# A decoder layer in float32 on one core: the input first, gate logits and two key tiles chunk by chunk in turn, and the per-layer embedding projection moved to the end

## The chip, the core and the metric

The kernel runs on one core of one Trainium2 chip. The metric is device time in microseconds (us) of one execution. The core has a matrix engine (TensorE, PE in the profile; its weight loads are listed apart as PEld), a vector engine (VectorE, DVE), a scalar engine (ScalarE, ACT), a general engine (GpSimd, POOL) and a sync engine (SP) that here issues all the DMA transfers. Each engine runs its own instruction list in order and waits for the others through semaphores. SBUF is the on-chip memory of 128 partitions, PSUM the memory into which PE writes, DRAM the memory off the core.

## What is computed

One layer of a hybrid decoder, for a prompt of 1024 tokens and 64 sample tokens (8 sequences of 8), with a model width of 1024, in float32. The reference, cut to what matters:

```python
proj = rmsnorm(h, norm_mix) @ w_in
qkv, z, b_logit, a_logit, sq, sk, sv, gates = jnp.split(proj, cuts, axis=-1)
o_a = gdn_branch(...)   # causal conv of width 4 + silu on q, k, v; l2norm of q and k;
                        # beta = sigmoid(b_logit), g = -exp(a_log)*softplus(a_logit + dt_bias);
                        # gated delta rule in chunks of 64 with a triangular solve; 8 heads
o_b = swa_branch(...)   # sliding-window attention, 16 heads of 64, window 128
h = h + (sigmoid(gates[:D]) * o_a + sigmoid(gates[D:]) * o_b) @ w_out
h = h + relu(rmsnorm(h, norm_ffn) @ w_up)**2 @ w_down
h = h + sigmoid(rmsnorm(h, norm_ple) @ w_ple_gate) * (p_l @ w_ple_proj)
```

The last line is the per-layer embedding: `p_l` (256 features a token) times `w_ple_proj` (256 by 1024) needs nothing but inputs, and is called PLE below.

## The kernel before

**Numbers and tiles.** Features lie on the partitions, tokens along the rows. The T = 1088 tokens are cut into chunks `CH` of 384, 384 and 320 columns; the 1024 features are KT = 8 tiles of 128, the k tiles. Each float32 operand is split in two rounded halves, x = xh + xl and w = wh + wl, and a product is three matmuls: xh by wh (L166), xl by wh (L167), xh by wl (L168). One output tile of 128 features (one f) is 8 k tiles x 3 chunks x 3 = 72 such matmuls.

**Weights.** A list `order` fixes the order in which weight tiles of 512 KB are streamed: `w_load` issues the DMA into `wr` (three buffers), `w_split` copies the high half on ACT (`wh`, L134) and subtracts on POOL (`wl`, L135; for the first two tiles on DVE), into two buffers each. `next_w` hands out a split tile and sets the next load and split going.

**Order.** The program is written for a tile scheduler that sets the order on each engine from the program text and the tiles' buffers. The start, however, is laid out by hand: a tuple of steps runs the eight PLE tiles `ple(0)` to `ple(7)` in between the steps of the three input norms n0, n1, n2.

**The start.** The inputs `pT` are loaded and split (`phi`, `plo`, L286 and L287). A PLE tile is 2 k tiles x 3 chunks x 3 = 18 matmuls (L166 to L168 with `phi` and `plo`), 144 for all eight. Each is copied out of PSUM by ACT, times 0.5, into `ppo` (L328; four buffers) and stored to DRAM (`ppd`, L332, 544 KB each). `x_norm(i)` handles chunk i of the input: ACT squares it (L306), DVE adds the eight k tiles up (L309), `rsqrt_pe` sums over the partitions by one-column matmuls (`psn`, L247), DVE scales (L250), POOL takes the power -0.5 (L251), DVE builds diagonal tiles (`dg`, L256), and PE spreads them over the partitions (`pst`, L257). Then per k tile DVE multiplies by the norm (L316), ACT rounds off the high half (`xh`, L317), POOL or, for two of eight, DVE subtracts (`xl`, L318).

**Gates, keys, solve.** After the norms come the gate logits `ba` (48 matmuls, L388), their transposes (L427), a chain of small DVE steps from logits to the decay `g` (L401 to L422), and PE's cumulative sums of g (L435 on). Then a loop over the eight heads h computes the key tile of each: `conv_steps` (72 matmuls, copies out of PSUM into `raw`, four conv steps on DVE with `cacc`, L511), `key_rows` (the decay rows `E`, one buffer) and `key_products` (k by k matmuls, L591, multiplied by E on DVE and copied by ACT into `kk` and `kb`, L593, stored to DRAM). After the last head DVE solves the triangular systems row by row (`fs`, L666, and `LT`, L667) while PE goes on with the projections of the attention; the attention's key and query halves (`klo`, L888; `qst`, L901) are DVE steps queued among the solve's rows, and PE's first score matmuls (`psc`, L930 and L931) read them.

**The end.** After the attention, the delta rule, `w_out` and the MLP (8 blocks; the last block's `w_down` tiles feed `next_operand`, which makes the last norm's operand `ph`, `pl`, with L200, and adds up squares in `acc`, L1388), the gate of the PLE is one projection: f = 0 to 7, 72 matmuls each. f = 0 runs its chunks in turn (`inter=True`) while `col_rsqrt_pe` makes the norm's scale from `acc`. Per f a buffer `B` is loaded from `ppd`, and per chunk DVE multiplies by the norm's scale (L1450), ACT takes the tanh (L1451), DVE multiplies by the PLE tile (L1452) and adds to h (L1454), and SP stores the result (L1455).

## Time and profile before

| what | value |
|---|---|
| time, median of 3 runs (lowest, highest) | 2139.82 us (2135.79, 2142.8) |
| the profiled execution: its own time | 2146.7 us |
| its span | 2144.9 us |
| TensorE clock granted, mean over the span | 0.983 of full speed |
| PE busy | 2079.6 us |
| DVE, ACT, POOL busy | 1071.9, 795.5, 718.0 us |
| DMA moved | 196.50 MB |

The profiled execution is one run: its time is 6.9 us above the median of the three, and its span lacks 1.8 us of its time. A row of a timeline has the start in us, the duration, the engine, the source line, the operation, the tiles written and read, how many instructions the row holds, and in brackets the idle time before it and what ended that. Matmuls overlap: the distance between the starts of two matmuls in a row is what one costs, not its duration.

### The profile page before, as it was taken

The numbers are of one execution on the slowest core, as the hardware profiler recorded it, in microseconds if no ns is written. First come the engines' busy times: TensorE is split into PE (matmuls) and PEld (weight loads), VectorE is DVE, ScalarE is ACT, GpSimd is POOL, SyncE is SP. The second block draws the span as 40 slices with busy tenths as digits, with TensorE's granted clock in tenths as the row PEclk, the third lists the DMA queues.
The fourth block names the chain that finished last, engine by engine and source line by source line (L and its number), as shares of the span: only waits on it lengthen the run. The fifth ranks groups of instructions, "written<-read, shape, count | busy, mean of one in ns | idle before, by whom it ended". The sixth has DMA issues, their size and how long they took to land.

```text
span 2144.9 us, 33830 instructions
## 1 busy us (share of the span) xinstructions
PE 2079.6 (97%) x13597; PEld 1995.2 (93%) x13597; DVE 1071.9 (50%) x1717; ACT 795.5 (37%) x1951; POOL 718.0 (33%) x676
## 2 busy tenths in 40 slices
PE   6999999789999999999999999999999999999999
PEld 6899899668889999999998999999999999999999
DVE  6444499787654555445555444233332323333654
ACT  6476433477643443344334322212131212212411
POOL 3332456243235545454455222212121212121211
PEclk9999999899999999999999999999999999999999
DMA  6365443343243223322242221111111111111132
GB/s 238 122 216 183 116 147 109 104 125 114 85 142 97 76 93 123 108 92 77 93 151 75 77 69 50 40 50 40 50 40 50 40 50 41 49 43 47 40 127 80
DMA packets 89065, 196.50 MB, mean 92 GB/s; under 512 B 33613, under 2 KB 44749, under 8 KB 88781
## 3 DMA queue, kind: packets, MB, share of 16 engines
q1 hardware_dynamic: 88908, 194.35, 27.7%
q8 instruction: 107, 1.75, 0.3%
q14 instruction: 50, 0.40, 0.1%
HBM read 145.48 MB, written 50.78 MB: 91 GB/s over the span
## 4 chain that ended last, share of the span: by engine, by line
PE 80%; DVE 11%; ACT 4%; issue 3%; POOL 2%; DMA 1%; SPq 0%; ACTq 0%; DVEq 0%; POOLq 0%
PE ps L166 23%; PE ps L168 22%; PE ps L167 22%; DVE fs L666 3%; DVE LT L667 3%; PE psn L975 1%; PE pst L953 1%; DVE nm L938 1%; PE psc L1285 1%; ACT pst L572 1%; PE psc L1216 1%; PE psn L1297 1%; PE psc L1290 1%; PE psc L1280 1%; ACT pr L940 1%
## 5 line engine op out<-in xcount | busy, mean ns | idle before, releaser
L135 POOL TENSOR_TENSOR wl<-wr,wh 128x1024 fp32r<-128x1024 f32 x140 | 343.4, 2453 | 909.1 <-ACT wh L134 893.8
L166 PE MATMUL ps<-xh,wh 128*128 128x384 f32 (+1 forms) x1800 | 621.9, 345 | 3.0 <-ACT qf L350 1.6
L167 PE MATMUL ps<-xl,wh 128*128 128x384 f32 (+1 forms) x1800 | 600.1, 333 | 0.0
L168 PE MATMUL ps<-xh,wl 128*128 128x384 f32 (+1 forms) x1800 | 596.7, 332 | 0.0
L166 PEld LDWEIGHTS ps<-xh,wh 128*128 128x128 f32 x1800 | 343.1, 191 | 15.9 <-issue 11.1
L167 PEld LDWEIGHTS ps<-xl,wh 128*128 128x128 f32 x1800 | 343.9, 191 | 1.2 <-issue 1.1
L168 PEld LDWEIGHTS ps<-xh,wl 128*128 128x128 f32 x1800 | 342.1, 190 | 1.6 <-issue 0.7
L134 ACT ACTIVATE wh<-wr 128x1024 fp32r<-128x1024 f32 x143 | 150.8, 1054 | 518.2 <-PE ps L167 441.3
L166 PE MATMUL ps<-uh,wh 128*128 128x384 f32 (+1 forms) x768 | 251.2, 327 | 1.2 <-DVE h L1436 1.2
L168 PE MATMUL ps<-uh,wl 128*128 128x384 f32 (+1 forms) x768 | 251.3, 327 | 0.0
L167 PE MATMUL ps<-ul,wh 128*128 128x384 f32 (+1 forms) x768 | 251.0, 327 | 0.0
L1436 DVE TENSOR_TENSOR h<-h,ps 128x384 f32<-128x384 f32 (+1 forms) x192 | 100.6, 531 | 226.3 <-PE ps L168 226.3
L166 PE MATMUL ps<-ph,wh 128*128 128x384 f32 (+1 forms) x600 | 197.9, 330 | 0.0
L167 PE MATMUL ps<-pl,wh 128*128 128x384 f32 (+1 forms) x600 | 197.6, 329 | 0.0
L168 PE MATMUL ps<-ph,wl 128*128 128x384 f32 (+1 forms) x600 | 197.5, 330 | 0.0
L1422 DVE TENSOR_TENSOR ul<-us,uh 128x384 fp32r<-128x384 f32 (+1 forms) x96 | 98.0, 1022 | 115.2 <-ACT uh L1421 115.2
L166 PEld LDWEIGHTS ps<-uh,wh 128*128 128x128 f32 x768 | 144.3, 188 | 2.0 <-DVE h L1436 2.0
L168 PEld LDWEIGHTS ps<-uh,wl 128*128 128x128 f32 x768 | 144.3, 188 | 0.0
L167 PEld LDWEIGHTS ps<-ul,wh 128*128 128x128 f32 x768 | 144.2, 188 | 0.0
L511 DVE SCALAR_TENSOR_TENSOR cacc<-raw,cw,cacc 128x1112 f32<-128x1112 f32 x72 | 111.1, 1543 | 62.0 <-ACT cacc L509 60.7
L1420 ACT ACTIVATE us<-ut 128x384 f32<-128x384 f32 (+1 forms) x96 | 48.2, 502 | 196.0 <-DVE ut L1419 194.5
L1419 DVE SCALAR_TENSOR_TENSOR ut<-ps,rb 128x384 f32<-128x384 f32 (+1 forms) x96 | 51.3, 535 | 136.5 <-PE ps L168 136.5
(413 smaller groups left out, 3410.4 us busy)
## 6 DMA issues: line engine op xcount, KB each, us to landing
wr<-win SPq DMA_DIRECT2D x60, 512.0 KB
wr<-wup SPq DMA_DIRECT2D x32, 512.0 KB
wr<-wdn SPq DMA_DIRECT2D x32, 512.0 KB
ppd<-ppo SPq DMA_DIRECT2D x8, 544.0 KB
kTd<-kT SPq DMA_DIRECT2D x8, 544.0 KB
Ed<-E SPq DMA_DIRECT2D x8, 544.0 KB
rg<-Ed SPq DMA_DIRECT2D x8, 544.0 KB
gkT<-kTd SPq DMA_DIRECT2D x8, 544.0 KB
```

The costliest lines, as they stand in the source:

```text
L134: act(hv, rv, AF.Copy)
L135: (nc.gpsimd if i > 1 else nc.vector).tensor_tensor(lv, rv, hv.bitcast(F32), ALU.subtract)
L166: mm(ps[:M, :w], a, h[:, c0 : c0 + w], start=(k == 0), stop=False)
L167: mm(ps[:M, :w], a, l[:, c0 : c0 + w], start=False, stop=False)
L168: mm(ps[:M, :w], b, h[:, c0 : c0 + w], start=False, stop=(k == n - 1))
L511: stt(out=cc, in0=raw[:, j : j + CONVW], scalar=cw[:, f, j : j + 1], in1=cc, op0=ALU.mult, op1=ALU.add)
L666: tt(tmp, X[:, j : j + 1, j + 1 :].broadcast_to(sh), X[:, 0:j, j : j + 1].broadcast_to(sh), ALU.mult)
L667: tt(X[:, 0:j, j + 1 :], X[:, 0:j, j + 1 :], tmp, ALU.add)
L1419: stt(out=t, in0=ps[:, :w], scalar=0.0, in1=rb2[:, c0 : c0 + w], op0=ALU.max, op1=ALU.mult)
L1420: act(s, t, AF.Square)
L1422: tt(lo[:, c0 : c0 + w], s, hi[:, c0 : c0 + w].bitcast(F32), ALU.subtract)
L1436: tt(hc, hc, ps[:, :w], ALU.add)
```

## The change

- **Weights.** The two PLE weight tiles `wpp` leave the head of the list and stand ahead of the last block's four `wdn` tiles; `wba` (the gate logits' weights) comes third, behind two key weights. Its split goes to a tile `wn` of its own. The PLE weights are split into buffers of the `xh` and `xl` kind, free by then.
- **Start.** SP issues chunk 0 of the input first, then the constants, one key weight, chunk 1, a key weight, chunk 2, `wba`. The PLE is gone from here. The norm n0 is followed by `turn(0)`, then n1, `turn(1)`, n2, `turn(2)`. A turn holds three PSUM tiles and for each of the 8 k tiles issues three matmuls for key tile 8, three for key tile 9 and two for the gate logits, all on chunk i (64 matmuls a turn, 192 in all). Then ACT copies the three tiles out. The key loop's first two heads do only what is left (`conv_rest`).
- **Key loop.** `E` has two buffers. `kb` is gone, ACT writes its copy into half of `kk`. `key_products` stands behind the loop's second step, not its first.
- **End.** `pT` is loaded and split in the last MLP block, behind the PLE weights. `ple(f)` writes its 18 matmuls' result into three PSUM tiles (two of `psc`, one of `pst`) that stay there; `ple(0)` stands ahead of `col_rsqrt_pe`, `ple(f)` ahead of the gate's tile f. The multiplication by the PLE tile reads PSUM; the factor 0.5 moves into the last addition, now a two-operation DVE step. The eight 544 KB stores to `ppd` and the eight loads from it are gone.

The diff, cut to its core:

```diff
-    order = [(d["wpp"][u], 1024) for u in range(2)] + [(d["wba"], 128)]
-    order += [(d["win"][f], 1024) for f in WIN_ORDER]
+    order = [(d["win"][f], 1024) for f in WIN_ORDER]
+    order.insert(2, (d["wba"], 128))
...
+        if b == NUP // 4 - 1:
+            ple_order = len(order)
+            order += [(d["wpp"][u], 1024) for u in range(2)]
+        order += [(d["wdn"][b, u], 1024) for u in range(4)]
...
+                if 0 <= i - ple_order < 2:
+
+                    hi, lo = (xp.tile([P, T], F32R, name=z, tag=t)[:, :1024] for z, t in (("wph", "xh"), ("wpl", "xl")))
...
+    ba = ep.tile([P, T], F32, name="ba", tag="qraw", bufs=1)[:32]
+    raw0 = [ep.tile([P, RAWW], F32, name="raw0", tag="tg") for _ in range(2)]
...
         for i, (c0, w) in enumerate(CH):
...
+            for k in (0, 4):
+                dma(x_in[i][:, k : k + 4], d["xT"][k : k + 4, :, c0 : c0 + w].rearrange("k p t -> p k t"))
+            if i == 0:
+                load_constants()
                 w_load()
...
+            else:
+                w_load()
+        dma(cache, d["cachec"])
...
-        for step in (0, 1, 2, n0, n1, n0, n0, 3, n1, n2, n1, 4, 5, n2, n2, 6, 7):
-            if isinstance(step, int):
-                ple(step)
-            else:
-                next(step, None)
...
+        next(n0)
+        w_split()
+        evacs = [conv_raw(8 + h, raw0[h]) for h in range(2)]
+        keys, (wb, _) = [next_w() for _ in range(2)], next_w()
+        next(n0)
+
+        def turn(i):
+            c0, w = CH[i]
+            c = slice(c0, c0 + w)
+            pk = [pg.tile([P, 512], F32, name="ps", tag="ps") for _ in range(2)]
+            pb = pg.tile([P, 512], F32, name="ps", tag="ps")
+            for k in range(KT):
+                x_h, x_l = (z[:, c] for z in xs[k])
+                for ps, (hi, lo) in zip(pk, keys):
+                    a, b = (z[:, k * P : k * P + P] for z in (hi, lo))
+                    mm(ps[:, :w], a, x_h, start=(k == 0), stop=False)
+                    mm(ps[:, :w], a, x_l, start=False, stop=False)
+                    mm(ps[:, :w], b, x_h, start=False, stop=(k == KT - 1))
+                for j, z in enumerate((x_h, x_l)):
+                    mm(pb[:32, :w], wb[:, k * 32 : k * 32 + 32], z, start=(k + j == 0), stop=(k + j == KT))
+            act(ba[:, c], pb[:32, :w], AF.Copy)
+            for f, ps in zip(evacs, pk):
+                f(c0, w, ps)
+
+        turn(0)
+        next(n1)
+        next(n1)
+        turn(1)
+        next(n2)
+        next(n2)
+        turn(2)
...
-        E = kp.tile([P, T], F32, name="E", tag="E", bufs=1)
+        E = kp.tile([P, T], F32, name="E", tag="E")
...
-        kb = kp.tile([P, 8, 64], F32, name="kb", tag="kb", bufs=1)
...
-            act(kb[64:128, hf * 4 : hf * 4 + 4], ps[64:128].rearrange("p (c f) -> p c f", f=P)[:, :, 0:64], AF.Copy)
+            act(kk[64:128, hf * 4 : hf * 4 + 4, 0:64], ps[64:128].rearrange("p (c f) -> p c f", f=P)[:, :, 0:64], AF.Copy)
...
+        if h < 2:
+            kT = conv_rest(8 + h, raw0[h], kp, key_tile)
+            continue
...
+            wpl, prhs = [next_w() for _ in range(2)], []
+            for k in range(2):
+                pr = B()
+                dma(pr, d["pT"][k])
+                hi = xp.tile([P, T], F32R, name="pph", tag="xh")
+                lo = xp.tile([P, T], F32R, name="ppl", tag="xl")
+                act(hi, pr, AF.Copy)
+                tt(lo, pr, hi.bitcast(F32), ALU.subtract)
+                prhs.append((hi, lo))
...
+    def ple(f):
+
+        res = []
+        for i, (c0, w) in enumerate(CH):
+            ps = pst() if i == 2 else psc()
+            for k, (h_, l_) in enumerate(prhs):
+                a, b = (z[:, k * 512 + f % 4 * P : k * 512 + f % 4 * P + P] for z in wpl[f // 4])
+                mm(ps[:, :w], a, h_[:, c0 : c0 + w], start=(k == 0), stop=False)
+                mm(ps[:, :w], a, l_[:, c0 : c0 + w], start=False, stop=False)
+                mm(ps[:, :w], b, h_[:, c0 : c0 + w], start=False, stop=(k == 1))
+            res.append(ps)
+        return res
+
+
+    first = ple(0)
     col_rsqrt_pe(acc, 1.0 / 1024, EPS, rb2, tp)
...
     for f in range(KT):
-        pr = B()
-        dma(pr, ppd[f])
+        pr = dict(zip((c0 for c0, _ in CH), ple(f) if f else first))
...
-            stt(out=t, in0=t, scalar=1.0, in1=pr[:, c0 : c0 + w], op0=ALU.add, op1=ALU.mult)
+            stt(out=t, in0=t, scalar=1.0, in1=pr[c0][:, :w], op0=ALU.add, op1=ALU.mult)
             hc = hT[f][:, c0 : c0 + w]
-            tt(hc, hc, t, ALU.add)
+            stt(out=hc, in0=t, scalar=0.5, in1=hc, op0=ALU.mult, op1=ALU.add)
```

Three places of the instruction order, before and now. Line numbers of the changed program differ: L257 and L267 there are the old L247 and L257, L394 to L396 the key matmuls, L398 the gate logits.

The first is PE's list where the norm of the second and third chunks is made. Before, the small norm matmuls of the third chunk stand singly among the PLE's matmuls (`phi`, `plo`):

```order
L166 MATMUL ps<-phi,wh 128x384
L257 MATMUL pst<-dg,cst 128x128 x2
L167 MATMUL ps<-plo,wh 128x384
L257 MATMUL pst<-dg,cst 128x64
L168 MATMUL ps<-phi,wl 128x384
```

Now the end of turn 0 and the start of turn 1 stand so:

```order
L394 MATMUL ps<-xh,wh 128x384
L395 MATMUL ps<-xl,wh 128x384
L396 MATMUL ps<-xh,wl 128x384
L398 MATMUL ps<-xh,wn 32x384
L398 MATMUL ps<-xl,wn 32x384
L257 MATMUL psn<-cst,xsq 128x1 x5
L257 MATMUL psn<-cst,xsq 64x1
L267 MATMUL pst<-dg,cst 128x128 x4
L394 MATMUL ps<-xh,wh 128x384 x2
```

The partition sums and the spreading of the second chunk's norm stand together between the turns, with no large matmul between the two.

The second is DVE's list in the triangular solve, where `klo` is queued. Before:

```order
L666 TENSOR_TENSOR fs<-LT 128x572
L667 TENSOR_TENSOR LT<-LT,fs 128x52x11
L666 TENSOR_TENSOR fs<-LT 128x530
L667 TENSOR_TENSOR LT<-LT,fs 128x53x10
L888 TENSOR_TENSOR klo<-klo,khi 128x1024
L666 TENSOR_TENSOR fs<-LT 128x486
```

Now (L681, L682, L903 and L949 are the old L666, L667, L888 and L934):

```order
L681 TENSOR_TENSOR fs<-LT 128x572
L903 TENSOR_TENSOR klo<-klo,khi 128x1024
L682 TENSOR_TENSOR LT<-LT,fs 128x52x11
L681 TENSOR_TENSOR fs<-LT 128x530
L949 SCALAR_TENSOR_TENSOR pr<-psc,rq,tab 128x128
L682 TENSOR_TENSOR LT<-LT,fs 128x53x10
```

`klo` moved ahead of three steps of the solve, and the first score step (`pr`) that follows from it stands two solve steps behind it.

The third is POOL's list ahead of `rks`, a power that the solve waits for. Before:

```order
L135 TENSOR_TENSOR wl<-wr,wh 128x1024 x2
L220 TENSOR_TENSOR nlo<-nsq,nhi 128x384 x2
L790 COPY vss<-vt 64x128
L220 TENSOR_TENSOR nlo<-nsq,nhi 128x320
L220 TENSOR_TENSOR nlo<-nsq,nhi 128x384 x2
L135 TENSOR_TENSOR wl<-wr,wh 128x1024
L220 TENSOR_TENSOR nlo<-nsq,nhi 128x320
L645 TENSOR_TENSOR rks<-rks,pwr 64x8
```

Now (L145, L230, L660 are the old L135, L220, L645):

```order
L145 TENSOR_TENSOR wl<-wr,wh 128x1024 x3
L230 TENSOR_TENSOR nlo<-nsq,nhi 128x384 x2
L805 COPY vss<-vt 64x128
L230 TENSOR_TENSOR nlo<-nsq,nhi 128x320
L230 TENSOR_TENSOR nlo<-nsq,nhi 128x384 x2
L230 TENSOR_TENSOR nlo<-nsq,nhi 128x320
L660 TENSOR_TENSOR rks<-rks,pwr 64x8
```

The weight split that stood two rows ahead of `rks` now stands ahead of all of the `nlo` rows.

More of the change, by code (lines that the diff above doesn't have):

```diff
@@ new lines, in conv_rest @@
+    def conv_rest(f, raw, cvp, dst):
+        rs = raw[:, 3 + NP :].rearrange("p (b t) -> p b t", t=11)
+        nc.gpsimd.tensor_copy(cstate[:, f, 0:3], raw[:, NP : NP + 3])
+        nc.gpsimd.tensor_copy(cstate[:, f, 3:27].rearrange("p (b t) -> p b t", t=3), rs[:, :, 8:11])
+        c = cvp.tile([P, RAWW], F32, name="cacc", tag="cacc", bufs=2)
+        cc = c[:, :CONVW]
+        act(cc, raw[:, 0:CONVW], AF.Copy, scale=cw[:, f, 0:1])
+        for j in range(1, 4):
+            stt(out=cc, in0=raw[:, j : j + CONVW], scalar=cw[:, f, j : j + 1], in1=cc, op0=ALU.mult, op1=ALU.add)
+        th = raw
+        act(th[:, :CONVW], cc, AF.Tanh, scale=0.5)
+        v = lambda z: z[:, NP + 3 : RAWW].rearrange("p (b t) -> p b t", t=11)[:, :, 0:8]
+        if callable(dst):
+            dst = dst()
+        if dst is None:
+            sg = cvp.tile([P, NS], F32, name="sg", tag="sg", bufs=2)
+            stt(out=sg.rearrange("p (b t) -> p b t", t=8), in0=v(th), scalar=1.0, in1=v(c), op0=ALU.add, op1=ALU.mult)
+            stt(out=c[:, :NP], in0=th[:, :NP], scalar=1.0, in1=c[:, :NP], op0=ALU.add, op1=ALU.mult)
+            return c, sg
+        stt(out=dst[:, :NP], in0=th[:, :NP], scalar=1.0, in1=c[:, :NP], op0=ALU.add, op1=ALU.mult)
+        stt(out=dst[:, NP:T].rearrange("p (b t) -> p b t", t=8), in0=v(th), scalar=1.0, in1=v(c), op0=ALU.add, op1=ALU.mult)
+        return dst
@@ L334, in hybrid_layer @@
[L334 to L351 removed]
+            yield
@@ L371, in hybrid_layer @@
     rq, rqs = mp.tile([P, 8, 2, 8], F32, name="rq"), mp.tile([P, NB], F32, name="rqs")
-    ectx = ctx.enter_context(ExitStack())
-    ep = pool(ectx, "ep", 2, side="right")
     kctx = ctx.enter_context(ExitStack())
```

136 lines of the change are left out of this document (42 added, 94 removed).

## The prediction, made before the changed kernel was run

> **What bounds the kernel now.** I read the page's busy times first, PE's list of waits in the start next, then the timelines of PE, ACT, DVE and POOL there, the waits later on, and last the final projection.
>
> ```profile
> PE 2079.6 (97%) x13597; PEld 1995.2 (93%) x13597; DVE 1071.9 (50%) x1717; ACT 795.5 (37%) x1951; POOL 718.0 (33%) x676
> ```
>
> PE is busy 97% of the span. The change removes no matmul: 144 PLE matmuls leave the start and 144 of the same kind come at the end. Only time that PE loses to waits, or to a lower clock, can be won or lost. The list of waits of PE in the first 90 us (us in total, times, longest) shows the losses in the start:
>
> ```profile
> PE ps L166 <- ACT wh L134: 6.7, 1, 6.7
> PE pst L257 <- DVE dg L256: 4.0, 2, 3.4
> PE ps L166 <- ACT ppo L328: 3.3, 1, 3.3
> PE pst L435 <- DVE lg L420: 1.7, 1, 1.7
> ```
>
> Waits cost more than their length, since the matmuls after them run slowly. PE's timeline around two waits, and the granted clock of 70 to 80 us (0.66):
>
> ```profile
> 36.42 0.34 PE L168 MATMUL ps<-phi,wl 128*128 128x384 f32 x1
> 36.60 0.35 PE L166 MATMUL ps<-phi,wh 128*128 128x384 f32 x1
> 37.28 0.30 PE L167 MATMUL ps<-plo,wh 128*128 128x320 f32 x1
> 37.42 0.31 PE L168 MATMUL ps<-phi,wl 128*128 128x320 f32 x1
> ...
> 47.45 1.20 PE L257 MATMUL pst<-dg,cst 128*128 128x128 f32 x4 [3.39 <-DVE dg L256]
> ...
> 52.88 0.48 PE L388 MATMUL ps<-xl,wh 128*32 128x384 f32 x1
> 53.19 0.34 PE L388 MATMUL ps<-xh,wh 128*32 128x384 f32 x1
> ...
> 60.84 0.71 PE L427 MATMUL pst<-cst,ba 32*128 32x32 f32 x6
> ...
> 69.82 0.41 PE L435 MATMUL pst<-g,cst 128*128 128x64 f32 x2 [1.68 <-DVE lg L420]
> ...
> 76.69 0.52 PE L168 MATMUL ps<-xh,wl 128*128 128x384 f32 x1
> 77.58 0.32 PE L166 MATMUL ps<-xh,wh 128*128 128x320 f32 x1
> ```
>
> ```profile
> 70.00:80.00 10.00, 10.00 (x47) 8.66 (x47) 1.81 (x10) 2.74 (x14) 0.00 (x0) 0.66 0.06 16
> ```
>
> Starts lie 0.175 us apart (36.42 to 36.60) for 384 columns and 0.145 for 320 at full clock, and 0.31 (52.88 to 53.19) for 384 in the slow stretches. Each us of slow stretch loses 1 - 0.175/0.31, about 0.45 us. After the 3.39 us gap at 47.45 PE is slow until 53.19, 5.7 us, so 2.6 lost; after the mere 1.68 at 69.82, which small matmuls follow, the last slow row is that of 76.69, another 7 us.
>
> **A: the first 192 large matmuls (+3.2).** Before, 144 PLE and 48 gate-logit matmuls end at 60.84. After, three turns of 64, with the same columns, hold two key tiles and the gate logits. So the two moments compare directly: 192 matmuls are 128 x 0.175 + 64 x 0.145, about 31.7 us at full clock, and before lost 29 of its 61 us. The PLE was what PE could do before the norms; now nothing can. The first rows of that chain, by their nearest rows before:
>
> ```profile
> 4.26 0.84 ACT L286 ACTIVATE phi<-praw 128x768 fp32r<-128x768 f32 x1 [2.26 <-DMA praw<-pT]
> 8.89 1.06 ACT L134 ACTIVATE wh<-wr 128x1024 fp32r<-128x1024 f32 x1 [0.46 <-DMA wr<-wpp]
> 10.98 1.48 ACT L306 ACTIVATE xsq<-xc 128x1536 f32<-128x1536 f32 x1
> 27.76 1.05 ACT L317 ACTIVATE xh<-xc 128x384 fp32r<-128x384 f32 x2 [2.23 <-DVE xc L316]
> ```
>
> ```profile
> 9.99 1.23 DVE L135 TENSOR_TENSOR wl<-wr,wh 128x1024 fp32r<-128x1024 f32 x1 [0.56 <-ACT wh L134]
> 15.51 3.35 DVE L309 TENSOR_TENSOR xsq<-xsq 128x1536 f32<-128x1536 f32 x3 [1.56 <-ACT xsq L306]
> 24.52 0.63 DVE L256 TENSOR_SCALAR dg<-cst,rcomp 128x128 f32<-128x128 f32 x2
> 27.11 1.66 DVE L316 SCALAR_TENSOR_TENSOR xc<-xc,par,pst 128x384 f32<-128x384 f32 x3
> ```
>
> ```profile
> 21.28 2.31 POOL L251 TENSOR_TENSOR rcomp<-rcomp,pwr 128x3 f32<-128x3 f32 x1 [20.86 <-DVE rcomp L250]
> 26.02 0.85 POOL L251 TENSOR_TENSOR rcomp<-rcomp,pwr 128x3 f32<-128x3 f32 x1 [2.43 <-DVE rcomp L250]
> 30.46 3.23 POOL L318 TENSOR_TENSOR xl<-xc,xh 128x384 fp32r<-128x384 f32 x3 [0.36 <-ACT xh L317]
> ```
>
> ```profile
> 25.02 0.73 PE L247 MATMUL psn<-cst,xsq 128*128 128x1 f32 x6
> ```
>
> By 4.26 one piece of `pT` (0.39 MB) had landed, by 8.89 two pieces and two weights (1.8 MB). Chunk 0 of the input is 1.57 MB: its first half is there at about 5.3, all at 8. Squares 1.48, to 9.7; adds 3.35, to 13; sums and scaling 0.9, to 14; the first power 2.3, to 16.3; `dg` twice 0.63, the key weight's split, which DVE's order puts ahead of the third `dg`, 1.23, the third 0.3, spreading 0.5: 19. Multiply and round, 0.55 and 0.52: the first `xh` at about 19.5 to 20. Key 9's weight then holds PE: ACT has it behind three `xh` and a square (to 23.5), DVE's half behind eight multiplications and one `xl` (19 + 8 x 0.55 + 0.6 = 24, and 1.23: 25). POOL's six `xl` at 1.1 each end by 27, ahead of need. So PE is dense from about 25 with 49 matmuls of turn 0 left: 8.5, and some 2 of slow clock as after the gap at 47.45, end at 35.5.
>
> Now the gap between turns: PE's order has the second chunk's partition sums only behind turn 0 and its spreading straight after, and nothing between. Sums 0.73, scaling 0.16, power 0.85, `dg` 0.63, spreading 0.4, multiply 0.55, round 0.52: 3.8 us. Turn 1 starts near 39.4 and takes 11.2 plus 2 slow: 52.5. Behind it stand the third chunk's last spreading and the logits' transposes, then multiply and round; 2 us. Turn 2, 64 x 0.145 = 9.3, ends at 64. That is 3.2 later than 60.84. I put no slow stretch behind the 2 us, since dense matmuls follow at once; the row of 69.82 says that there may be one, and it would cost 2 to 3. Ends: 61 (no slow clock in turns 1 and 2) to 68 (dense from 27, each turn slow for 5.7).
>
> [...]
>
> **B: gates and the first two keys (+2.6).** The group of conv steps, and two rows of POOL, from the solve's start:
>
> ```profile
> L511 DVE SCALAR_TENSOR_TENSOR cacc<-raw,cw,cacc 128x1112 f32<-128x1112 f32 x72 | 111.1, 1543 | 62.0 <-ACT cacc L509 60.7
> ```
>
> ```profile
> 251.14 2.40 POOL L135 TENSOR_TENSOR wl<-wr,wh 128x1024 fp32r<-128x1024 f32 x1 [2.35 <-ACT wh L134]
> ...
> 254.33 1.63 POOL L645 TENSOR_TENSOR rks<-rks,pwr 64x8 f32<-64x8 f32 x1
> ```
>
> Before, PE takes from 60.84 to 77.58 for 48 key matmuls (8.4 us) and about 2 us of small ones: 6.4 lost to the gates. After, key tiles 8 and 9 are done, so PE starts with head 2: its weight waits for a buffer that turn 2 frees (`wh` 1.06, `wl` on POOL 2.40, part of it covered: 1.8); the first key products wait for a conv chain that used to run beside 72 matmuls (1.3); the gates' small steps share DVE with six conv steps of 1.54, so g comes later (2.3) and a slow stretch follows (2.5). With about 1 of smaller waits that is 9 lost, 2.6 more than before. Ends: -2 (head 2 covers all) and +5 (each in full, two slow stretches).
>
> **C: key loop and solve (-4.1).** PE's waits from 61 to 400 us:
>
> ```profile
> PE psc L931 <- DVE klo L888: 7.1, 1, 7.1
> PE psc L591 <- ACT kb L593: 2.6, 2, 1.7
> PE psc L930 <- DVE qst L901: 2.0, 1, 2.0
> ```
>
> ```profile
> 385.21 0.75 DVE L667 TENSOR_TENSOR LT<-LT,fs 128x572 f32<-128x572 f32 x1
> ...
> 386.74 0.71 DVE L667 TENSOR_TENSOR LT<-LT,fs 128x530 f32<-128x530 f32 x1
> ```
>
> `kb`'s waits are those on the copy out of PSUM. Two `E` buffers and the later place of `key_products` can take all 2.6 or none: half, -1.3. The 7.1 + 2.0 before `klo` and `qst` are DVE's queue: DVE is full with the solve, so `klo` comes when the solve's rows ahead of it are done. `klo` moves ahead of three of these (first and last shown, the one between is a multiplication as long as the last): 0.75 + 0.71 + 0.71 = 2.2. The solve waits for `rks`; the 2.40 split that stood before it now stands earlier: up to 2.4. Of 4.6 I take 60%, -2.8, since the third split now holds up `nlo`, which PE's norms wait for. Ends -7.2 and 0.
>
> **D: the end (+0.5).** Of PE's timeline, the first row of gate tile f = 0, the wait in it, and f = 1:
>
> ```profile
> 2034.07 0.34 PE L166 MATMUL ps<-ph,wh 128*128 128x384 f32 x1
> ...
> 2040.13 0.83 PE L247 MATMUL psn<-cst,acc 128*128 128x1 f32 x6 [1.04 <-DVE acc L1388]
> ...
> 2056.71 0.36 PE L166 MATMUL ps<-ph,wh 128*128 128x384 f32 x1
> ```
>
> f = 0 takes 22.6 us for work of 11.9: 10.7 lost, of which only 1.04 is one wait; the rest is small norm matmuls and the slow clock among them. `ple(0)`, 18 matmuls or 3 us, now stands ahead of that and could cover it. But the eight `xh` buffers are now filled by the four operand tiles of the last block's `w_down` and by four of the PLE (two of inputs, two of weights), so the operands of f = 5 to 7 for the gate, which are of that kind, can be written only when the last `w_down` tile has been read. I put them and the sum `acc` 1.5 to 2.5 later; then `ple(0)`'s 3 us are used up and the 10.7 stay. `ple(1)`'s PSUM tiles wait for f = 0's evacuation, 0 to 1.9. The eight stores and eight loads of 544 KB lay beside a busy PE; without them nothing is saved. The multiplication by 0.5 that goes was on ACT, the one that comes rides in DVE's last addition, 0.55 either way. If `acc` isn't later, D is -3; if the buffers hold up PE, +3.
>
> **Sum.** 3.2 + 2.6 - 4.1 + 0.5 = +2.2. The profiled execution took 2146.7 (span 2144.9 and 1.8 around it) and would take 2148.9; it lies 6.9 above the median 2139.82, and from that the forecast is 2142.
>
> **Rivals.**
> - *Turns in full series (slower).* Each norm waits for the turn before, each turn starts slow, and B's waits add up: A +7, B +5, C -4.1, D +0.5: +8.4, 2148. For it: PE's order, and a slow clock after only 1.68 us of idle. Against it: the squares and additions of the later chunks are done early. It decides when turn 2 ends after 67 us.
> - *Shorter waits behind the start (faster).* A 0, B 0, C -7.2, D -1: -8.2, 2132. For it: 9.1 us of waits for DVE's queue, whose order moved the right way. Against it: PE's late start, which no other work covers.
> - *`ple(0)` covers the last norm (faster).* A, B, C as forecast, and D -6 in place of 0.5: -4.3, 2135.5. For it: 3 us of work at full clock ahead of the sums, which keep PE busy while `acc` ends. Against it: the small norm matmuls stay spread among the large ones, and `acc` comes later.
>
> **Chances.** 0.3% of this time, 6.4 us, is about what a measurement can tell from no change. Forecast 0.44 (its terms' ends leave 0.33 within 0.3%, 0.08 slower, 0.03 faster), turns in series 0.26 (0.20 slower, 0.06 within), shorter waits 0.22 (0.19 faster, 0.03 within), covered norm 0.08 (0.05 within, 0.03 faster). That is faster 0.25, within 0.47, slower 0.28. The range runs from rival two's 2132 to rival one's 2148, and beyond each by 2 and 4, the scatter of the three runs (4.0 below and 3.0 above the median): 2130 to 2152.
>
> **What would show it.** In the profile of the changed kernel: first dense turn matmuls near 25, turn 2's end near 64, a gap of 3.8 between turn 0 and 1 with slow pitch after it, the wait on `klo` near 4 in place of 7.1, and 10 to 11 us lost in f = 0. I am wrong if turn 2 ends before 60 or after 68, or if the sum of PE's waits behind 100 us moves by over 6.

## The result: slower by 0.8%, and the profile after

| what | before | after |
|---|---|---|
| median of 5 runs each, side by side on one chip | 2141.92 us | 2158.26 us |
| ratio, with its 95% interval | | 1.0078 [1.0053, 1.0103] |
| the same in two later comparisons | | 1.0056 [1.0035, 1.0078], 1.0069 [1.0045, 1.0093] |
| profiled execution, its span | 2146.7, 2144.9 us | 2160.68, 2158.9 us |

The kernel became 12 to 16 us slower; +2.2 was forecast, and 2158 lies outside the forecast's range. One run of the changed kernel, in the last comparison, took 4041.35 us, and its medians here leave that run out. The busy times of after, for the line shown of before:

```profile
PE 2081.2 (96%) x13597; PEld 1994.9 (92%) x13597; DVE 1069.2 (50%) x1716; ACT 787.5 (36%) x1926; POOL 728.6 (34%) x676
```

PE has the same 13597 matmuls and as good as the same busy time: 1.6 us more, while the span grew by 14.0. What came in this pair of profiles is idle time. The longest of PE's waits of after in its first 100 us (us in total, times, longest):

```profile
PE psn L257 <- DVE xsq L367: 12.3, 1, 12.3
PE ps L395 <- POOL xl L375: 2.7, 1, 2.7
PE ps L394 <- ACT xh L374: 2.6, 3, 1.3
PE pst L267 <- DVE dg L266: 2.4, 4, 1.5
PE ps L398 <- POOL wn L145: 1.2, 1, 1.2
PE ps L178 <- POOL wl L145: 1.0, 1, 1.0
```

PE's timeline of after at the landmarks that the prediction named: the first large matmul, the two waits on POOL, the ends of turn 0 (the `psn` row) and turn 1 (the `pst` row at 56.49), the starts of turns 1 and 2, the last matmul of turn 2, and the last two of the logits' eight transposes behind it.

```profile
18.88 0.69 PE L394 MATMUL ps<-xh,wh 128*128 128x384 f32 x1 [1.26 <-ACT xh L374]
...
26.59 0.65 PE L395 MATMUL ps<-xl,wh 128*128 128x384 f32 x1 [2.75 <-POOL xl L375]
...
33.32 0.36 PE L398 MATMUL ps<-xh,wn 128*32 128x384 f32 x1 [1.23 <-POOL wn L145]
...
38.74 0.72 PE L257 MATMUL psn<-cst,xsq 128*128 128x1 f32 x6
...
43.60 0.91 PE L394 MATMUL ps<-xh,wh 128*128 128x384 f32 x2 [0.70 <-ACT xh L374]
...
56.49 0.74 PE L267 MATMUL pst<-dg,cst 128*128 128x128 f32 x4
...
58.38 0.56 PE L394 MATMUL ps<-xh,wh 128*128 128x320 f32 x2 [0.66 <-ACT xh L374]
...
68.10 0.31 PE L398 MATMUL ps<-xl,wn 128*32 128x320 f32 x1
69.04 0.31 PE L475 MATMUL pst<-cst,ba 32*128 32x32 f32 x2 [0.64 <-ACT ba L399]
```

The first large matmul came at 18.88, a little before the forecast's 19.5 to 20. But turn 0 ended at 38.7 (35.5 was forecast), and from there every landmark is 3 to 4 us behind the forecast. The 192 matmuls end at 68.25; before, they ended at 60.84, where the transposes started. (Of these, six stand between turns 1 and 2 now; the last two wait 0.64 us for a copy, until 69.04.) POOL's and DVE's timelines of after in turn 0 show why:

```profile
21.21 1.01 POOL L375 TENSOR_TENSOR xl<-xc,xh 128x384 fp32r<-128x384 f32 x1 [0.56 <-ACT xh L374]
22.57 9.15 POOL L375 TENSOR_TENSOR xl<-xc,xh 128x384 fp32r<-128x384 f32 x4 [0.35 <-ACT xh L374]
31.67 0.94 POOL L301 COPY raw<-cache 128x24 f32<-128x24 f32 x2
32.57 0.69 POOL L145 TENSOR_TENSOR wn<-wr,wn 128x128 fp32r<-128x128 f32 x1
```

```profile
23.46 0.55 DVE L375 TENSOR_TENSOR xl<-xc,xh 128x384 fp32r<-128x384 f32 x1
23.93 9.02 DVE L367 TENSOR_TENSOR xsq<-xsq 128x1536 f32<-128x1536 f32 x6
```

Four subtractions of POOL, 1.01 us each a moment earlier, take 9.15 (2.29 each) while DVE, from 23.93 on, adds up the squares of chunks 1 and 2. DVE's six additions take 9.02 there; without POOL beside them they take 5.8 (below). The two engines hold each other up, and `wn` is queued behind. At 21.21 DVE was at work too, but with multiplications (L373, five in 2.71 us from 19.70) one input of which, `pst`, lies in PSUM.

The kernel before has the same in small, in rows that the prediction did not use. POOL's subtractions, 1.08 us each at 30.46, take 1.9 at 34.06, where DVE adds (the other rows are DVE's):

```profile
34.06 3.83 POOL L318 TENSOR_TENSOR xl<-xc,xh 128x384 fp32r<-128x384 f32 x2
33.70 1.76 DVE L309 TENSOR_TENSOR xsq<-xsq 128x1280 f32<-128x1280 f32 x1
35.91 1.10 DVE L309 TENSOR_TENSOR xsq<-xsq 128x640 f32<-128x640 f32 x1
```

Later in the program, PE's waits from 100 to 400 us and from 1300 to 2060 us:

```profile
PE psc L946 <- DVE klo L903: 6.5, 1, 6.5
PE pst L550 <- ACT pst L585: 2.4, 3, 1.2
PE psc L603 <- ACT kk L605: 2.1, 2, 1.7
PE ps L178 <- POOL wl L145: 1.6, 2, 0.9
```

```profile
PE ps L177 <- DVE ul L1437: 2.3, 1, 2.3
PE ps L176 <- DVE h L1461: 0.8, 2, 0.4
PE psn L257 <- DVE acc L1403: 0.2, 1, 0.2
```

The wait on `klo` hardly shrank (7.1 to 6.5), the waits on the copies became 2.1 in place of 2.6 and others of 2.4 (0.4 before) and 1.6 stand beside them, and the MLP has a wait that before did not have.

**Where the time is lost.** To compare stretches that hold different matmuls, I took for each stretch its time minus what its own matmuls need at the distances that such matmuls have in dense rows at full clock. How high a figure comes out hangs on the distance taken for the small matmuls; the differences between the columns change by a us or so at most. In us, by profile; "moved alone", "mended" (chunk 0's `xl` and `wn` on DVE) and "three mended" are experiments below:

| stretch, up to | before | before again | PLE moved alone | after | after again | mended | three mended |
|---|---|---|---|---|---|---|---|
| transposes of the betas | 31.1 | 28.6 | 42.7 | 37.7 | 38.7 | 32.8 | 33.3 |
| end of the key loop | 10.8 | 11.2 | 9.9 | 13.7 | 13.7 | 14.5 | 16.5 |
| first score matmul (`khi`) | 22.5 | 23.2 | 22.4 | 19.1 | 17.7 | 17.7 | 17.7 |
| first `klo` | 7.6 | 5.6 | 5.2 | 6.8 | 6.7 | 6.7 | 6.7 |
| end of the attention | 83.9 | 82.7 | 82.8 | 89.8 | 88.9 | 85.7 | 88.1 |
| start of the delta rule | 7.5 | 9.0 | 8.7 | 9.9 | 11.4 | 11.3 | 9.8 |
| its rest and `w_out` | 80.7 | 78.0 | 81.6 | 80.9 | 77.9 | 77.9 | 81.5 |
| end of the MLP | 5.8 | 5.8 | 9.0 | 7.7 | 9.2 | 9.3 | 5.3 |
| gate tile f = 0 | 7.4 | 3.4 | 2.5 | 5.0 | 2.5 | 2.5 | 2.4 |

### The profile page after: what moved, and what is told of

It is laid out like the page before. It is cut to its first block, busy times and chain, and to the rows that moved or that the text cites. A ratio compares the mean times of both kernels' runs of the same rounds, so it can differ in the third digit from the quotient of the medians.

```text
span 2158.9 us, 33737 instructions
## 1 busy us (share of the span) xinstructions
PE 2081.2 (96%) x13597; PEld 1994.9 (92%) x13597; DVE 1069.2 (50%) x1716; ACT 787.5 (36%) x1926; POOL 728.6 (34%) x676
## 3 DMA queue, kind: packets, MB, share of 16 engines
q8 instruction: 107, 1.75, 0.3%
## 4 chain that ended last, share of the span: by engine, by line
PE 74%; DVE 3%; ACT 2%; POOL 1%; issue 1%; DMA 0%; SPq 0%; ACTq 0%; POOLq 0%; DVEq 0%
PE ps L176 21%; PE ps L178 20%; PE ps L177 20%; PE psn L990 1%; PE pst L968 1%; PE psc L1300 1%; PE psc L1231 1%; PE psn L1312 1%; DVE nm L953 1%; PE psc L1305 1%; PE psc L1295 1%; PE pst L1167 1%; DVE pr L949 1%; PE psn L1316 1%; PE psc L945 1%
## 5 line engine op out<-in xcount | busy, mean ns | idle before, releaser
L145 POOL TENSOR_TENSOR wl<-wr,wh 128x1024 fp32r<-128x1024 f32 x138 | 338.9, 2456 | 867.7 <-ACT wh L144 852.5
L176 PE MATMUL ps<-xh,wh 128*128 128x384 f32 (+1 forms) x1752 | 601.6, 343 | 3.9 <-ACT qf L294 1.6
L178 PE MATMUL ps<-xh,wl 128*128 128x384 f32 (+1 forms) x1752 | 579.2, 331 | 2.6 <-POOL wl L145 2.6
L177 PE MATMUL ps<-xl,wh 128*128 128x384 f32 (+1 forms) x1752 | 580.6, 331 | 0.0
L176 PEld LDWEIGHTS ps<-xh,wh 128*128 128x128 f32 x1752 | 331.9, 189 | 16.2 <-issue 10.2
L178 PEld LDWEIGHTS ps<-xh,wl 128*128 128x128 f32 x1752 | 331.3, 189 | 5.4 <-POOL wl L145 3.5
L177 PEld LDWEIGHTS ps<-xl,wh 128*128 128x128 f32 x1752 | 332.5, 190 | 1.3 <-issue 1.0
```

The source lines that it names most:

```text
L145: (nc.gpsimd if i > 1 else nc.vector).tensor_tensor(lv, rv, hv.bitcast(F32), ALU.subtract)
L176: mm(ps[:M, :w], a, h[:, c0 : c0 + w], start=(k == 0), stop=False)
L177: mm(ps[:M, :w], a, l[:, c0 : c0 + w], start=False, stop=False)
L178: mm(ps[:M, :w], b, h[:, c0 : c0 + w], start=False, stop=(k == n - 1))
```

## The experiments

Ratios are to the kernel before, run beside it; medians of before were 2143.89 (beside the PLE moved alone, the PLE in front, the key loop's edits), 2138.16 (the old key loop, the two with the norm inside a turn, `ppl` alone), 2143.03 (the late input, `xl` alone, `xl` with `ppl`, the changed kernel again), 2142.51 (`kb` apart, `xl` with `wn`) and 2143.21 (all three, the changed kernel a third time).

**The kernel before again.** A second profile, to see what one profile is worth.

> The kernel before once more, for the trace: how much the losses of PE by stretch differ between two executions of one kernel. Theory (the attention stretch loses 6 us more in the changed kernel by its own waits): from the first klo score to the first gkT row the loss is 84 +-1 again. Rival (slow-clock windows fall by chance): it differs by 3 us or more and the slow time with it.

Measured: 2136.9. The mean clock of the two profiles, before's first and then the second's:

```profile
core 0: 2144.9 us, clock 0.983
```

```profile
core 0: 2135.1 us, clock 0.988
```

By the clock records the lower clock was granted for 76.5 us in the first and 54.5 in the second. The 22.0 us between, at 0.45 lost per us, are 9.9, as good as the 9.8 by which the spans differ. So a single stretch of a single profile proves nothing below about 4 us; verdicts rest on medians, and on rows that repeat.

**The PLE moved to the end, alone.** The kernel before with the input first and the PLE at the end as in the change; no turns, the old key loop.

```diff
-        for step in (0, 1, 2, n0, n1, n0, n0, 3, n1, n2, n1, 4, 5, n2, n2, 6, 7):
+        for step in (n0, n1, n0, n0, n2, n1, n1, n2, n2):
```

> The kernel before with one part of the change: the input first and the embedding projection moved to the end (PSUM, last block's loads), no turns, the key loop as before. Theory (lost cover): the 144 projection matmuls were what PE did while the norms ran. Without them the gate logits end near 46 us where before they end at 60.84 with 23.8 us more work behind them, so the start loses 9 us more; the end gains 2 as in the changed kernel: +5 to +9 against before. Rival (key loop edits are the cause of the slowdown): -3 to +1, since the key loop is the old one. Rival (the turns are the cause): also near 0.

Measured: 2157.97, ratio 1.0067 [1.0045, 1.009], as much as the whole change. Its waits in the first 100 us:

```profile
PE psn L254 <- DVE xsq L303: 12.4, 1, 12.4
PE ps L364 <- POOL xl L312: 4.8, 7, 1.7
PE ps L364 <- ACT xh L311: 3.8, 4, 1.4
```

PE does nothing until 12.4, then follows the operands one by one. 42.7 us are lost in the start in place of 31.1 or 28.6, and the whole is 14.1 slower, more than the 5 to 9 expected. The turns get part of the start's loss back (37.7). It is not the missing cover alone: POOL's first six subtractions stand among DVE's additions here too (from 20 to 30 us POOL is busy for 9.27 with six steps, DVE for 9.96), and PE's waits for POOL's `xl` add up to 4.8; and the MLP loses 9.0 in place of 5.8.

**Turns, but the PLE in front.** To give the cover back, the PLE's steps stand among the norms again and the three turns behind them. `ppo` has two buffers here and `xsq` one.

```diff
+        for step in (0, 1, 2, n0, n1, n0, n0, 3, n1, n2, n1, 4, 5, n2, n2, 6, 7):
...
-            sq = pp.tile([P, KT, 384], F32, name="xsq", tag="xsq", bufs=2)[:, :, :w]
+            sq = pp.tile([P, KT, 384], F32, name="xsq", tag="xsq", bufs=1)[:, :, :w]
```

> The changed kernel with the embedding projection put back in front, among the norms, and through DRAM (two buffers for its copies, one for the squares), then the three turns with all of the input normed, and the new key loop. Theory (lost cover): the start's loss goes back by 5 to 7 us, the end's gain of 2 and the last block's stall of 2 go too: 2151 to 2153, that is +8 to +11 against before where the changed kernel is at +16. Rival (key loop edits or turns are the cause): it stays within 3 us of the changed kernel, +13 to +17.

Measured: 2166.81, ratio 1.0109 [1.0088, 1.013]. It has new waits on `xsq` (7.5 us) and `dg` (10.9) in the start; that they come from the buffers that were cut is likely, not shown. So it tells nothing of the cover.

**The key loop's edits alone, on the kernel before.**

```diff
-        E = kp.tile([P, T], F32, name="E", tag="E", bufs=1)
+        E = kp.tile([P, T], F32, name="E", tag="E")
...
-            act(kb[64:128, hf * 4 : hf * 4 + 4], ps[64:128].rearrange("p (c f) -> p c f", f=P)[:, :, 0:64], AF.Copy)
+            act(kk[64:128, hf * 4 : hf * 4 + 4, 0:64], ps[64:128].rearrange("p (c f) -> p c f", f=P)[:, :, 0:64], AF.Copy)
```

`next(st)`, the loop's next conv step, moves ahead of `key_products`, as in the change.

> The kernel before with the key loop's edits alone: two E buffers, one tile kk for both copies, key products behind the second step. Theory (lost cover in the start): -1 to +2 against before, PE's idle time between 75 and 215 us about as before, 3.7 us. Rival (the key loop edits cost the 3 us that the key phase loses in the changed kernel): +3 to +5, idle 7 us there.

Measured: 2140.66, ratio 0.9992 [0.9976, 1.0008]: no change. The key loop loses 15.1 in place of 10.8, the solve's start 14.7 in place of 22.5.

**The same with `kb` kept apart.**

> The kernel before with two E buffers and key_products behind the loop's second step; kb stays a tile of its own. Nothing else of the change. With kk and kb in one tile as well the ratio was 0.9992 [0.9976, 1.0008]: 4.3 us more were lost in the key loop than in the kernel before, and 7.8 us less at the solve's start. Theory that the loss in the key loop comes from the merged tile (the DVE half and the ACT half of one tile, stored by one transfer, hold each other's buffer): with kb apart the loss in the key loop returns to 10 to 12 us, the gain at the solve's start stays, and the ratio is 0.996 to 0.998. Rival, that the loss comes from the later place of key_products itself (copies and products bunch behind the second step): the key loop loses 14 to 15 us again, ratio 0.998 to 1.0005.

Measured: 2146.22, ratio 1.0013 [0.9997, 1.0028]; 16.1 lost in the key loop, 17.9 at the solve's start. My theory of the merged tile fell, the rival stands. PE's waits in the key loop (75 to 218 us), the kernel before again first:

```profile
PE psc L591 <- ACT kb L593: 2.6, 2, 1.7
PE pst L537 <- ACT pst L572: 0.4, 2, 0.2
```

```profile
PE pst L537 <- ACT pst L572: 5.4, 7, 1.8
PE pst L532 <- DVE kT L522: 2.4, 3, 1.4
```

The wait on `kb` goes, and waits on ACT's copies and on `kT`, seven and three of them, take its place.

**The change with the old key loop.**

```diff
-        E = kp.tile([P, T], F32, name="E", tag="E")
+        E = kp.tile([P, T], F32, name="E", tag="E", bufs=1)
```

and `kb` and the old place of `key_products` with it.

> The changed kernel with the old key loop (one E buffer, kb, key products behind the first step). In its instruction order PE's 72-matmul tiles are spread among the first scores of the attention as before (107 of them done at the 16th score, where the changed kernel has 130 to 137 and then none left). Theory (the order of the fillers costs the attention 6 us): the stretch from the first klo score to the first gkT row goes from 90 back to 83 to 84 us of loss, and the total to 2149 to 2154. Rival (slow-clock windows by chance): that stretch stays at 87 to 90 and the total within 3 us of the changed kernel, 2155 to 2161.

Measured: 2165.33, ratio 1.0122 [1.01, 1.0143]. At the solve's start 32.2 are lost in place of 19.1, 6.4 of it in one wait on `qf`. The changed kernel lies 11.9 to 16.3 above the kernel before and this one 27.2, so beside the turns these edits earn some 11 to 15 us, and nothing without them. The attention loses 86.7 here, so neither the 83 to 84 of the theory nor its total came.

**The next norm started inside a turn.** Behind k = 3 of a turn stand the next chunk's sums and spreading; then the same with the old key loop.

```diff
             for k in range(KT):
...
+                if k == 3:
+                    yield
```

> The changed kernel with each later chunk's norm started in the middle of the turn before it (behind the fourth k tile), so that its sums and spreading stand among the turn's matmuls. Theory (the bare gap between the turns): turn 2 ends 4 to 6 us earlier, near 63; the attention's fillers are used up even earlier in the order, so that stretch stays at 90 or a little above; 2152 to 2156. Rival (POOL's and ACT's halves of x set the pace of the turns, not the gap): turn 2 ends at 66 to 68, total 2156 to 2161.

> Both: norms inside the turns and the old key loop; PE's order in the attention is again that of before. Theory (start's gap and the fillers' order each cost their part): start 5 less, attention 6 less than the changed kernel: 2144 to 2150, within 0.3% of before. Rival (chance or a cause that neither edit touches): 2153 or more.

Measured: 2165.08, ratio 1.0119 [1.0097, 1.0142], and 2165.74, 1.0124 [1.0103, 1.0145]. The spreading now stands inside the turns, the logits' last transposes come at 65.5 in place of 69.0, and the start loses 34.1 in place of 37.7; but the first then loses 19.6 in the key loop (13.7) and 95.7 in the attention (89.8). The second has the attention's old order of filler matmuls and 87.3 there, and 31.1 at the solve's start. Both totals lie 9 us or more above what their theories had. What a step wins in the start is no gain if the order of what follows moves with it.

**The input a megabyte later.** Two key weights are issued ahead of chunk 0.

```diff
+            w_load()
+            w_load()
             for k in (0, 4):
```

> The changed kernel with two key weights (1 MB) issued ahead of the input's first chunk. At 352 GB/s they delay it by 3.0 us. Theory (PE has no cover ahead of the first xh, so the chain to it lies on the path and its delay goes through to the end): first xh 2.5 to 3 us later, 21.5, and the total 2 to 3 us over the changed kernel. Rival (what the start wins or loses is given back at the gates and in the key loop, whose conv chain on DVE sets the pace): first xh later, total within 1 us.

Measured: 2157.85, ratio 1.0075 [1.0049, 1.01]. (The 352 GB/s are what the kernel before moved from 10 to 20 us.) The first large matmul starts at 22.25, 3.4 later, and the end of the profile is 4.2 later than in the changed kernel beside it; the medians differ by 2.9. This fits a delay of the start that passes whole to the end; the two intervals overlap, so it is not proven.

**Chunk 0's subtractions on DVE.** First the eight `xl` alone, then `wn` too, so that POOL has nothing of turn 0.

```diff
-                (nc.vector if k % 4 == 0 else nc.gpsimd).tensor_tensor(lo, x[:, k], hi.bitcast(F32), ALU.subtract)
+                (nc.vector if k % 4 == 0 or i == 0 else nc.gpsimd).tensor_tensor(lo, x[:, k], hi.bitcast(F32), ALU.subtract)
...
-            (nc.gpsimd if i > 1 else nc.vector).tensor_tensor(lv, rv, hv.bitcast(F32), ALU.subtract)
+            (nc.gpsimd if i > 2 else nc.vector).tensor_tensor(lv, rv, hv.bitcast(F32), ALU.subtract)
```

> The changed kernel with all eight low halves of chunk 0 on DVE, ahead of the additions for chunks 1 and 2 (before: six on POOL, 2.29 us each while DVE adds, 1.0 to 1.2 else). Theory (DVE's additions and POOL's subtractions slow each other, and that makes turn 0 late): PE's waits for xl (2.75) and wn (1.2) in turn 0 go, turn 0 ends 3 to 4 us earlier, near 35; of that 1 to 4 reach the end, 2154 to 2157 where the changed kernel has 2158. Rival (DVE was the bound, and now adds later): turn 0 ends earlier, but turn 1 starts no earlier than 43, total 0.

> The changed kernel with chunk 0's eight low halves (xl) and the gate logits' weight subtraction (wn) both on DVE; nothing of the first turn is left on POOL. With only the xl moved, POOL's wn subtraction took 6.35 us beside DVE's additions, and turn 0 ended at 40.0 us. Theory that POOL is held up by DVE's long additions: with both moved the wait on wn (4.76 us there) goes, turn 0 ends at 35 to 36.5 (38.7 in the changed kernel), and the gates stage is reached 2 to 3.5 us earlier; the median is 2 to 4 us under the changed kernel's 2154.9 in its last comparison, ratio to the kernel before 1.004. Rival, that the start has no cover and each norm chain sets the end of its turn: turn 0 ends earlier, but turn 1 starts when the second chunk's spreading is there (43 us), turn 2 still ends at 67 to 68, and the time is that of the changed kernel within 2 us.

Measured: with `xl` alone 2159.85, ratio 1.0073 [1.0048, 1.0097]; with both 2150.34, 1.0047 [1.0027, 1.0066]. With `xl` alone POOL's one remaining step of the turn, and PE's wait on it:

```profile
26.09 6.35 POOL L145 TENSOR_TENSOR wn<-wr,wn 128x128 fp32r<-128x128 f32 x1 [4.65 <-ACT wn L144]
```

```profile
32.50 0.53 PE L398 MATMUL ps<-xh,wn 128*32 128x384 f32 x1 [4.76 <-POOL wn L145]
```

A subtraction of 0.69 us took 6.35 beside DVE's additions, and turn 0 ended at 40.1. The total gained nothing: the changed kernel beside it had 2154.92. With both moved, DVE's row of additions and `wn`, and PE's landmarks (starts of turn 0, of the second norm's sums, of turn 1, the end of turn 1, the last transposes):

```profile
25.82 1.75 DVE L367 TENSOR_TENSOR xsq<-xsq 128x1536 f32<-128x1536 f32 x1
27.49 0.28 DVE L145 TENSOR_TENSOR wn<-wr,wn 128x128 fp32r<-128x128 f32 x1
27.70 1.02 DVE L375 TENSOR_TENSOR xl<-xc,xh 128x384 fp32r<-128x384 f32 x2
28.63 4.08 DVE L367 TENSOR_TENSOR xsq<-xsq 128x768 f32<-128x768 f32 x5
```

```profile
18.89 0.69 PE L394 MATMUL ps<-xh,wh 128*128 128x384 f32 x1 [1.26 <-ACT xh L374]
...
32.65 0.72 PE L257 MATMUL psn<-cst,xsq 128*128 128x1 f32 x6
...
37.50 1.01 PE L394 MATMUL ps<-xh,wh 128*128 128x384 f32 x2 [0.70 <-ACT xh L374]
...
51.57 0.74 PE L267 MATMUL pst<-dg,cst 128*128 128x128 f32 x4
...
64.12 0.31 PE L475 MATMUL pst<-cst,ba 32*128 32x32 f32 x2 [0.64 <-ACT ba L399]
```

The same additions take 1.75 + 4.08 = 5.8. Turn 0 takes 13.8 us in place of 19.9 and ends at 32.65, turn 1 starts 6 us earlier, not at 43 as the rival had it, and the last transposes stand at 64.12. The contention was most of the price; a step of DVE's is shorter too, 0.55 us where POOL's takes 1.01 without DVE's additions beside it.

**The embedding's subtraction (`ppl`) on POOL.** In the changed kernel DVE's timeline in the last MLP block reads:

```profile
1976.57 2.60 DVE L1452 TENSOR_TENSOR ppl<-B,pph 128x1088 fp32r<-128x1088 f32 x1 [0.72 <-ACT pph L1451]
1979.09 0.54 DVE L1461 TENSOR_TENSOR h<-h,ps 128x384 f32<-128x384 f32 x1
1979.55 3.27 DVE L1452 TENSOR_TENSOR ppl<-B,pph 128x1088 fp32r<-128x1088 f32 x1
1982.75 0.48 DVE L1437 TENSOR_TENSOR ul<-us,uh 128x320 fp32r<-128x320 f32 x1
...
1994.31 1.28 DVE L1403 TENSOR_TENSOR acc<-acc,B 128x1088 f32<-128x1088 f32 x1
```

`ul`, for which PE waits 2.3 us, stands behind 5.9 us of `ppl`. An addition of the same size takes 1.28 at 1994.31, where POOL does nothing; beside the `ppl` POOL subtracts for weight splits (2.40 from 1975.61, 2.39 from 1979.29). So more than half of the 5.9 looks like the contention of turn 0 again, with DVE as the one that is held. The edit, with the changed kernel, with the `xl` edit, and with both edits of before (`xl` and `wn`):

```diff
-                tt(lo, pr, hi.bitcast(F32), ALU.subtract)
+                nc.gpsimd.tensor_tensor(lo, pr, hi.bitcast(F32), ALU.subtract)
```

> The changed kernel with the low half of the projection's input made on POOL, not on DVE. Theory (DVE's two such steps hold up ul in the last block): PE's wait on ul, 2.3 us, goes; -1 to -2 against the changed kernel, 2156 to 2157. Rival (ul is late for ACT's copies ahead of it): the wait stays, 0.

> The changed kernel with both edits: chunk 0's low halves on DVE and the projection's low halves on POOL. Theory (the terms add): 2.3 from the last block and 1 to 4 from the start, 0.35 to 0.6% over before. It still has no cover ahead of the first xh, so it stays slower than before by 7 us or more. Rival (no cover is not what costs): it comes within 0.2% of before.

> The changed kernel with chunk 0's low halves and the wn subtraction on DVE, and the subtraction for the embedding input's low half (ppl) at the end on POOL. Theory that the costs add: the start's gain of the first two (turn 0 ends at 32 to 33 us in place of 38.7, 4.6 us of the median) and the 3 to 4 us lost in the MLP's last blocks to ppl both go: 6 to 9 us under the changed kernel in the same comparison, ratio to the kernel before 1.002 to 1.0035, that is still no faster than it, since the 6 us or so that the start still lacks of cover stay. Rival, that only the start counts (the MLP wait was taken back elsewhere): 3 to 5 us under the changed kernel.

Measured: 2151.42, ratio 1.0058 [1.0035, 1.0081], within what the changed kernel itself shows; 2154.41, 1.0057 [1.0034, 1.008], 5.4 under the `xl` edit alone but only 0.5 under the changed kernel beside it; all three 2148.81, 1.0022 [1.0007, 1.0037]. The MLP loses 5.3 in all three profiles, a little less than in the kernel before (5.8).

**The changed kernel again**, beside two of the batches.

> The changed kernel once more, on the chip of the three that follow, for the trace and as their base. Theory (the attention stretch differs by chance, since a kernel with the same order there lost 85.6): its loss there is anything from 85 to 90 and its idle time 15.8 to 18.4; the start loses 37 to 39 again; time 0.6 to 0.9% over before. Rival (the 90 is this order's own): 89 to 90.

> The changed kernel again, for a comparison on the same chip. Both theories: ratio to the kernel before 1.0055 to 1.008, turn 0 ends at 38.7 us.

Measured: 2154.92, ratio 1.0056 [1.0035, 1.0078], and 2156.51, 1.0069 [1.0045, 1.0093]. Beside the latter the three mended places together are worth 7.7 us, as was forecast for costs that add, and 5.6 of 13.3 are left. No kernel tried is measurably faster than the kernel before.

## Why the prediction was wrong

By its own steps, after's profile against before's, which is 14.0 longer:

- **A, the first 192 matmuls: +7.4 (60.84 to 68.25) for +3.2.** The step that failed is "POOL's six `xl` at 1.1 each end by 27, ahead of need". They ended at 31.7 and `wn` at 33.3, PE waited 2.75 and 1.23, and a slow stretch from 27 to 30 followed. I had taken the price from a row of POOL in which DVE did not add beside it, though the change puts the six additions of chunks 1 and 2 right there. With POOL out of the turn A measures 63.32 - 60.84 = +2.5 (+3.0 in the kernel with all three mended), near the forecast's figure, though by other parts: turn 0 ends 2.9 earlier than forecast, the gap is 4.9 in place of 3.8 and turn 1 takes 14.1 in place of 13.1. What I left out is what DVE's additions and POOL's subtractions cost each other here: 2.29 in place of 1.01 for an `xl` in the changed kernel, and 6.35 in place of 0.69 for `wn` with `xl` alone moved; the 6.35 spans several of DVE's instructions, not one.
- **The gap between the turns** was there, 4.9 us from 38.74 to 43.60 with small matmuls in it, and after's clock records are slow from 43.7 to 47.1 behind it, as forecast; that costs some 1.5. Behind the shorter gap at 56.49 they are not.
- **B, gates and first keys: about -0.8 for +2.6.** The start as a whole lost 6.6 more, of which A is 7.4. `wl` did keep PE waiting, but 1.0 us, with 3.4 us of slow clock from 71.0 on; the other waits did not come.
- **C, key loop: +2.9 for -1.3.** The second half of "all 2.6 or none" was too kind: other waits came in place of the one removed. **Solve and `klo`: -4.2** (22.5 to 19.1 and 7.6 to 6.8) for -2.8. The place was wrong: the wait on `klo` fell by 0.6; the gain lies ahead of it, and the experiments tie it to the key loop's edits.
- **D, the end: -2.4 for +0.5** in f = 0, within what two profiles of one kernel differ there (7.4 and 3.4). `acc`'s wait fell from 1.04 to 0.2, which fits the third rival (`ple(0)` covers it), though not the -6 that it put on that.
- **Not in the sum at all: the MLP, +1.9 to +3.5.** The sum moved the PLE's matmuls to the end and left out the two `ppl` subtractions that go with them, 5.9 us on DVE ahead of a step for which PE waits. All profiles with the PLE at the end and `ppl` on DVE show 7.7 to 9.3 there, all with it on POOL, or with the PLE in front, 5.3 to 5.8.
- **Not in the sum, and the largest miss: the attention and the start of the delta rule, +8.3** (83.9 to 89.8, 7.5 to 9.9), which the sum put at nothing. The traces say what it consists of: in the attention PE is idle for 18.4 us in place of 16.1 and the lower clock is granted for 17.3 in place of 9.3, and 2.3 + 0.45 x 8.0 is the 5.9; the delta rule's start has 0.9 more idle and 3.4 more slow (the second profile of before has these 3.4 too). All profiles with turns lose 85.5 to 95.7 in the attention, with 12.6 to 21.3 us of slow clock, the five without 82.7 to 84.7, with 7.8 to 14.3. Why the clock falls more often there is open. The order of the fillers may have a part (95.7 where it moved most), but the changed kernel's own order gave anything from 85.5 to 92.9; with the old key loop it is the old order, and 86.7 and 87.3 are lost all the same, with the old gaps and more slow clock.

So beside the forecast's +2.2, A is 4.2 worse, the key loop 4.2, the MLP 1.9 and the attention with the delta rule's start 8.3; B, the solve and D give back 3.4, 1.4 and 2.9. Only the first and the MLP have a cause that experiments removed.

The rival "turns in full series" was to decide when turn 2 ends after 67, and it ended at 68.25; but its own mechanism, turns that wait for norms, is not what did it: the late one was turn 0, and it waited for POOL. Both signs that the prediction named for being wrong came: turn 2 ends after 68, and PE's waits behind 100 us add up to 47.8 in place of 40.9.

What remains of the change with the three places mended, 5.6 us, has no single place: the start still loses 2 to 5 more, the key loop 5 to 6, the attention 4 to 5, and some 5 come back at the solve's start. That taking the cover away costs time is shown by the move alone (+14.1, with some contention and the `ppl` steps in it); how much of that is cover, and that the mended kernel's remainder in the start is that same cover, is argued, not shown.

## What to carry to other kernels

Before work that needs only inputs is moved away from a start, count what PE will do until the first chain is through: here 12.3 us of nothing in place of 6.7, and in the one trial a start 3.4 us later came out as a median 2.9 later. A price from a row holds only for the neighbours that the row had (1.01 became 2.29 here): look what the other of VectorE and GpSimd will be doing at the new place, and ask of each instruction of a moved step, small ones too, who stands behind it. Look also whether the profile that you read the price from has a dearer row of the same step: here it had. An edit that brings nothing alone (the key loop's) can be needed beside another, so take a change apart in both directions.

## What the runs showed of the hardware

- POOL beside DVE, both subtracting or adding float32 tiles in SBUF: POOL's 128x384 step takes 2.29 us in place of 1.01, DVE's six additions 9.02 in place of 5.8, and one POOL step of 0.69 took 6.35. Of the 9.02, DVE's own part is 5.8; of the 9.15, POOL's is 4.0: together 9.8, and both were done in the 10.4 from 22.57 to 32.95, so the two worked nearly in turn. In the MLP it is DVE that is held: 2.60 and 3.27 for a subtraction of 128x1088 beside POOL's splits, where an addition of that size takes 1.28; and one and the same step of that size (`pl`, L210) takes 2.50 at 1991.88 beside a split of 2.41 on POOL (from 1990.83), but 1.35 at 1985.64, where POOL does nothing.
- The clock records of the first profile of before and of after have two levels, full speed and 0.5 of it. Every stretch at 0.5 that ends within the span lasts 3.41, 6.83, 10.24 or 13.65 us (11 such stretches before, 12 after). How much time falls slow differs from run to run: the two profiles of before have 76.5 and 54.5 us of it, and at 0.45 lost per us that accounts for the 9.8 us by which their spans differ.
